# First MLP product by seven block products instead of eight, its result kept in DRAM

## The chip, the cores and the metric

The kernel runs on one core of a Trainium2 chip, as one launch. The metric is the device time in microseconds (us). Three runs of the kernel before took 3506.61 to 3510.11 us, with a median of 3507.81.

## The reference, cut to what matters

Two layer types work one after the other on x of 1024 tokens by 1024 features: `first_block` (two hybrid layers) and `second_block` (one layer with four branches, their merge and an MLP). Only the end of the second layer is touched:

```python
def rms_norm(x, gain): ...      # x * rsqrt(mean(x*x) + eps) * gain, over the features
...
    merged = merged + gate * (branches[i] @ w_branch_up[i])    # four branches
    x = x + rms_norm(merged @ w_out, norm_mix_post)

    h2 = rms_norm(x, norm_mlp_pre)
    u = jax.nn.relu(h2 @ w_mlp_in)                   # 1024 x 1024 by 1024 x 4096
    x = x + rms_norm((u * u) @ w_mlp_out, norm_mlp_post)   # by 4096 x 1024
```

## The kernel before

**Layout and products.** Everything is held transposed: a tile has 128 features (partitions) by 512 tokens, so that 1024 tokens are two halves. Each operand of a product is split into a high and a low part (`split`: ScalarE, written ACT, rounds the high part; VectorE, DVE, subtracts it from the source, which leaves the low part), and each product of two tiles is three matmuls, high by high, high by low and low by high (`mm3`, lines 113 to 115). `fm` adds such triples over the k tiles into one PSUM tile named `mm`. Weights come in blocks of 512 KB (128 x 1024) through `wload`: SP issues the load into `raw` (two buffers), ACT casts it to `whi` (line 104) and DVE subtracts it to `wlo` (line 105), each with two buffers too. `rnorm` makes a norm's scale for 512 tokens: TensorE (PE) adds a column of squares over the partitions (`tp`, line 198), DVE scales it (line 140), GpSimd (POOL) takes the root (line 141), PE spreads it over the partitions (`pv`, line 206).

**The stages at the end.** `merge` makes the four up-products and the gates, `proj` makes merged @ w_out for one half, and `norms` (before's lines 1797 to 1806) does the rest for that half: for each of eight tiles it loads a tile of the old x (`xo`, line 1802, two buffers), scales the product (line 1803, DVE), adds it to `xo` (line 1804, DVE), stores the new x as `x3` in DRAM (line 1805); after the eight, `norm_half` squares and adds them (lines 186 to 190), takes a second `rnorm`, and scales (line 219) and splits them to the operand H of the MLP.

**The MLP before.** `mlp` runs over eight chunks of 512 hidden features. In a chunk `hidden` makes four f tiles of h2 @ w_mlp_in for both halves, each tile 8 k x 3 = 24 matmuls of 128 x 512; ACT copies it (line 1840), DVE does max(t, 0)·t (line 1841) and it is split into M tiles. `project` then multiplies those by four blocks of w_mlp_out and adds each result to Y (line 1862, DVE; the first chunk is copied by ACT, line 1860). Nothing of u goes to DRAM. `finish` makes the last norm, adds x3 and stores out_t (lines 1881 to 1883). The two products are 32 x 2 x 24 = 1536 matmuls each.

**What sets the order.** The order of each engine's instructions is fixed when the kernel is built, by a scheduler that may take an instruction earlier or later than its place in the text; each engine then works its list in order. SP's list holds nearly all DMA issues, the weight loads, `xo` loads and stores among them. A DMA issue that has to wait for a buffer or for data holds up all that stands behind it in SP's list.

## Time and profile before

| What | us |
| --- | --- |
| Median of three runs | 3507.81 |
| Profiled execution, its own time | 3508.32 |
| Span of its instructions | 3506.5 |
| Last root of `norms` (half 1) to the last matmul of the MLP | 2776.0 to about 3486 of the span |
| Tail after the last matmul | 20.5 |

A profile lists for each engine what it did and when. PE is the matmul engine, PEld its weight loads, DVE VectorE, ACT ScalarE, POOL GpSimd, SP the engine that issues DMAs (SPq its queue). A busy figure counts the time in which an instruction of the engine is in flight; matmuls overlap, so that their mean duration is longer than the distance from the start of one to the start of the next. The granted clock says at what share of its full speed (2.4 GHz) TensorE was let run.

### The profile page before, as it was taken

The numbers are of one execution on the slowest core, as the hardware profiler recorded it, in microseconds if no ns is written. First come the engines' busy times: TensorE is split into PE (matmuls) and PEld (weight loads), VectorE is DVE, ScalarE is ACT, GpSimd is POOL, SyncE is SP. The second block draws the span as 40 slices with busy tenths as digits, with TensorE's granted clock in tenths as the row PEclk, the third lists the DMA queues.
The fourth block names the chain that finished last, engine by engine and source line by source line (L and its number), as shares of the span: only waits on it lengthen the run. The fifth ranks groups of instructions, "written<-read, shape, count | busy, mean of one in ns | idle before, by whom it ended". The sixth has DMA issues, their size and how long they took to land.

```text
span 3506.5 us, 45207 instructions
## 1 busy us (share of the span) xinstructions
PE 3369.9 (96%) x18181; PEld 2812.7 (80%) x18181; DVE 1966.9 (56%) x3418; ACT 1321.3 (38%) x2106; POOL 109.2 (3%) x132
## 2 busy tenths in 40 slices
PE   7999999999999999999999999999989899999997
...
GB/s 185 57 36 51 50 55 57 140 179 86 48 43 36 41 46 63 158 162 119 87 95 65 67 55 56 49 70 75 85 256 178 158 89 48 48 49 49 49 61 149
DMA packets 138707, 302.34 MB, mean 86 GB/s; under 512 B 23944, under 2 KB 41336, under 8 KB 137984
## 3 DMA queue, kind: packets, MB, share of 16 engines
...
q8 instruction: 143, 2.34, 0.3%
...
## 4 chain that ended last, share of the span: by engine, by line
PE 83%; DVE 5%; issue 5%; ACT 3%; DMA 3%; POOL 1%; SPq 0%; DVEq 0%; POOLq 0%; ACTq 0%
PE mm L113 21%; PE mm L114 21%; PE mm L115 21%; PE lg L388 2%; PE lg L389 2%; PE tp L512 2%; PE pv L113 1%; PE pv L206 1%; PE pv L114 1%; PE pv L115 1%; DMA S<-mix 1%; PE tp L198 1%; DVE wlo L105 1%; PE tp L1392 1%; ACT whi L104 1%
## 5 line engine op out<-in xcount | busy, mean ns | idle before, releaser
L113 PE MATMUL mm<-H,whi 128*128 128x512 f32 x2400 | 958.2, 400 | 26.9 <-DVE S L369 5.0
L115 PE MATMUL mm<-H,wlo 128*128 128x512 f32 x2400 | 949.4, 396 | 5.9 <-DVE wlo L105 5.7
L114 PE MATMUL mm<-H,whi 128*128 128x512 f32 x2400 | 949.8, 396 | 2.1 <-DVE H L105 2.1
L104 ACT CAST whi<-raw 128x1024 fp32r<-128x1024 f32 (+1 forms) x340 | 334.4, 984 | 860.3 <-PE mm L114 768.7
L105 DVE TENSOR_TENSOR wlo<-raw,whi 128x1024 fp32r<-128x1024 f32 (+1 forms) x340 | 387.4, 1140 | 421.6 <-ACT whi L104 409.9
L113 PEld LDWEIGHTS mm<-H,whi 128*128 128x128 f32 x2400 | 456.5, 190 | 125.5 <-ACT H L107 7.2
L115 PEld LDWEIGHTS mm<-H,wlo 128*128 128x128 f32 x2400 | 455.7, 190 | 104.2 <-DVE wlo L105 12.3
L114 PEld LDWEIGHTS mm<-H,whi 128*128 128x128 f32 x2400 | 456.2, 190 | 92.7 <-DVE H L105 2.9
L113 PE MATMUL mm<-whi,H 128*128 128x256 f32 x960 | 277.2, 289 | 3.9 <-DVE S L576 3.2
L114 PE MATMUL mm<-wlo,H 128*128 128x256 f32 x960 | 274.6, 286 | 3.1 <-DVE wlo L105 3.1
L115 PE MATMUL mm<-whi,H 128*128 128x256 f32 x960 | 273.7, 285 | 0.0
L113 PE MATMUL mm<-M,whi 128*128 128x512 f32 x640 | 249.5, 391 | 1.7 <-ACT whi L104 1.5
L115 PE MATMUL mm<-M,wlo 128*128 128x512 f32 x640 | 249.7, 390 | 0.2 <-DVE wlo L105 0.2
L114 PE MATMUL mm<-M,whi 128*128 128x512 f32 x640 | 249.5, 390 | 0.0
L113 PEld LDWEIGHTS mm<-whi,H 128*128 128x128 f32 x960 | 184.6, 192 | 6.8 <-issue 4.2
L114 PEld LDWEIGHTS mm<-wlo,H 128*128 128x128 f32 x960 | 184.8, 193 | 5.1 <-DVE wlo L105 4.2
L115 PEld LDWEIGHTS mm<-whi,H 128*128 128x128 f32 x960 | 184.6, 192 | 0.4
L489 DVE CUSTOM_DVE_ANT_0 lg<-lg,strip 128x1024 f32<-128x1024 f32 x128 | 155.2, 1234 | 25.8 <-PE lg L389 25.6
L1862 DVE TENSOR_TENSOR Y<-Y,mm 128x512 f32<-128x512 f32 x112 | 77.0, 687 | 159.1 <-PE mm L115 159.0
L493 ACT ACTIVATE L<-lg,mx 128x1024 f32<-128x1024 f32 x128 | 142.7, 1118 | 36.5 <-DVE mx L489 30.3
L113 PEld LDWEIGHTS mm<-M,whi 128*128 128x128 f32 x640 | 120.2, 188 | 28.0 <-ACT whi L104 1.9
L115 PEld LDWEIGHTS mm<-M,wlo 128*128 128x128 f32 x640 | 120.5, 188 | 25.6 <-DVE wlo L105 0.6
...
## 6 DMA issues: line engine op xcount, KB each, us to landing
raw<-in_w_in SPq DMA_DIRECT2D x106, 512.0 KB, 3.6
raw<-in_w_out SPq DMA_DIRECT2D x48, 512.0 KB, 4.0
raw<-in_w_gate SPq DMA_DIRECT2D x46, 512.0 KB, 3.5
raw<-in_w_mlp_in SPq DMA_DIRECT2D x40, 512.0 KB, 3.3
raw<-in_w_mlp_out SPq DMA_DIRECT2D x40, 512.0 KB, 3.2
...
```

The costliest lines, as they stand in the source:

```text
L104: nc.scalar.copy(hi, src)
L105: nc.vector.tensor_tensor(out=lo, in0=src, in1=hi.bitcast(F32), op=ALU.subtract)
L113: mm(out, lh, rh, start=start, stop=False)
L114: mm(out, lh, rl, start=False, stop=False)
L115: mm(out, ll, rh, start=False, stop=stop)
L198: self.nc.tensor.matmul(ss[:, n * i + j:n * i + j + 1], acc[:, j * P:(j + 1) * P], self.one, start=True, stop=True)
L388: mm(out, Q[m][qb // 4][:, sl], KH[m][half][:, o:o + kn], start=True, stop=False)
L389: mm(out, Q[m][qb // 4][:, sl], KL[m][half][:, o:o + kn], start=False, stop=not more)
L489: nc.vector.tensor_tensor_reduce(out=lg, in0=lg, in1=strip[:, w0:w0 + 1024], op0=ALU.add, op1=ALU.min, scale=-1.0, scalar=3.0e38, accum_ou ...
L493: nc.scalar.activation(pm, lg, AF.Exp, bias=mx, scale=-1.0, accum_out=sm)
L512: nc.tensor.transpose(tp[:, j, :], pm[:, kb * P:(kb + 1) * P], self.ident)
L1862: nc.vector.tensor_tensor(out=Y[d][half], in0=Y[d][half], in1=pt, op=ALU.add)
```

## The change

**First product.** The first MLP product is done in blocks. For a pair g of f tiles (f1 = 2g, f2 = 2g + 1; 16 pairs), the weights are a 2 x 2 matrix of blocks A11, A12 (f1, k tiles 0 to 3 and 4 to 7), A21, A22 (f2), and the operand is a 2 x 2 matrix B11, B21 (half 0, k tiles 0 to 3 and 4 to 7), B12, B22 (half 1). Seven block products of 4 k x 3 = 12 matmuls replace eight: A11·B11, A12·B21, S2·T2, S1·T1, S3·T3, A22·T4, S4·B22, with S1 = A21 + A22, S2 = S1 − A11, S3 = A11 − A21, S4 = A12 − S2 made on DVE for each pair (`side_weights`), and T1 = B12 − B11, T2 = B22 − T1, T3 = B22 − B12, T4 = T2 − B21 made once (`side_sums`, T1 and T2 on DVE, T3 and T4 on POOL). Each S, T, A22 is then split into high and low. DVE puts the products together with seven adds a pair (`add`).

**Order in the text.** For the first E = 8 pairs, A11·B11 and A12·B21, which need half 0 only, stand in a loop of their own between the steps of `norms` for half 1; this stretch is called stage A here. The main loop then does S2·T2 and the rest for all 16 pairs (and A11·B11 and A12·B21 for the last eight).

**u in DRAM.** `relu2` is now ACT twice (Relu, Square), and u goes to DRAM by 64 stores of 256 KB from SP. The second product runs over four chunks of 1024 rows, for which `inner` loads the 16 tiles of u again and splits them; the w_mlp_out blocks are laid out for that. In the last chunk all of half 0 comes ahead of half 1.

**norms.** The sum with `xo` is done by POOL instead of DVE (line 1815 in the new text), the squares are added as each tile is finished, and the scaling is one DVE instruction (line 1825) ahead of the plain split. The tail's tiles (`Y`, `M`, `xo`) share one pool of 54 buffers named S.

The diff, cut:

```diff
@@ norms
-            r = self.rnorm(acc, 1.0 / 1024.0)
-            for f in range(8):
-                xo = self.T("xo", 2)
-                nc.sync.dma_start(out=xo, in_=self.x2[f * P:(f + 1) * P, hs])
...
-                nc.vector.tensor_tensor(out=ys[f], in0=ys[f], in1=xo, op=ALU.add)
-                nc.sync.dma_start(out=self.x3[f * P:(f + 1) * P, hs], in_=ys[f])
-            res.append(self.norm_half(ys, self.n2[:, 16:24]))
+            order = [0, 4, 1, 5, 2, 6, 3, 7]
...
+            def add(fs):
+                for f in fs:
+                    xo = self.T("xo", 2)
+                    nc.sync.dma_start(out=xo, in_=self.x2[f * P:(f + 1) * P, hs])
+                    nc.vector.scalar_tensor_tensor(out=ys[f], in0=ys[f], scalar=self.n2[:, 8 + f:9 + f], in1=st["r"], op0=ALU.mult, op1=ALU.mult)
+                    nc.gpsimd.tensor_tensor(out=ys[f], in0=ys[f], in1=xo, op=ALU.add)
+                    nc.sync.dma_start(out=self.x3[f * P:(f + 1) * P, hs], in_=ys[f])
+                    self.sumsq_add(st["acc"], ys[f], f == 0)
...
+            def scale(fs):
+                for f in fs:
+                    X[f] = self.T("Y", 16)
+                    nc.vector.scalar_tensor_tensor(out=X[f], in0=ys[f], scalar=self.n2[:, 16 + f:17 + f], in1=st["r2"], op0=ALU.mult, op1=ALU.mult)
+                n2(half, fs, X)
+            pairs = [order[2 * i:2 * i + 2] for i in range(4)]
+            return X, [first] + [lambda p=p: add(p) for p in pairs] + [second] + [lambda p=p: scale(p) for p in pairs]
@@ new functions
+    def side_sums(self, b11, b21, b12, b22, use):
...
+        nc.vector.tensor_tensor(out=t1, in0=b12, in1=b11, op=ALU.subtract)
+        nc.vector.tensor_tensor(out=t2, in0=b22, in1=t1, op=ALU.subtract)
+        use("T2", t2)
+        use("T1", t1)
+        nc.gpsimd.tensor_tensor(out=t3, in0=b22, in1=b12, op=ALU.subtract)
+        use("T3", t3)
+        nc.gpsimd.tensor_tensor(out=t4, in0=t2, in1=b21, op=ALU.subtract)
+        use("T4", t4)
+        use("B22", b22)
...
+    def side_weights(self, src1, src2, whole):
...
+        if whole:
+            W["A11"], W["A12"] = self.block_weights(raw[0], 4)
+        s1 = sm(a21, a22, ALU.add)
+        s2 = sm(s1, a11, ALU.subtract)
+        part("S2", s2)
+        part("S1", s1)
+        part("S3", sm(a11, a21, ALU.subtract))
+        part("A22", a22)
+        part("S4", sm(a12, s2, ALU.subtract))
+        return W
@@ mlp, first product
+        def relu2(f, half, t):
+            u = self.T("ht", 2)
+            nc.scalar.activation(u, t, AF.Relu)
+            nc.scalar.activation(u, u, AF.Square)
+            nc.sync.dma_start(out=ud[f][half], in_=u)
...
+        for g in range(E + 1):
+            if g < E:
...
+                w11, w12 = self.block_weights(raw, 4)
+                S1[g] = copied(self.prod(w11, XS["B11"]))
+            if last is not None:
+                c11(*last)
+            last = (g, S1[g], w12) if g < E else None
+            for _ in range(2 if g in (0, 3) else 1):
+                if todo:
+                    todo.popleft()()
...
+        W = weights(0)
+        for g in range(NG):
+            f1, f2 = 2 * g, 2 * g + 1
+            s1 = S1[g] if g < E else copied(self.prod(W["A11"], XS["B11"]))
+            w = add(s1, self.prod(W["S2"], XS["T2"]))
+            if g >= E:
+                c11(g, s1, W["A12"])
+            t = add(w, self.prod(W["S1"], XS["T1"]))
+            p7 = self.prod(W["S3"], XS["T3"])
+            add(w, p7, w)
+            relu2(f2, 1, add(t, p7))
+            nextw = weights(g + 1) if g + 1 < NG else None
+            relu2(f2, 0, add(w, self.prod(W["A22"], XS["T4"]), w, ALU.subtract))
+            relu2(f1, 1, add(t, self.prod(W["S4"], XS["B22"]), t))
+            W = nextw
@@ mlp, second product
+            for k in range(8):
+                t = self.T("Y", 16)
+                nc.sync.dma_start(out=t, in_=ud[8 * ch + k][half])
+                hi, lo = (self.hpage(), self.hpage()) if half == 0 else (self.T("M", 32, F32R), self.T("M", 32, F32R))
+                self.split(hi, lo, t)
...
+        for ch in range(4):
+            U = [inner(ch, half) for half in range(2)]
+            if ch == 3:
+                break
             for d in range(8):
...
+                w = wload2(ch, d)
+                for half in range(2):
+                    project(ch, d, w, U[half], half)
```

**Order on SP in stage A.** First the rows of before, behind the first root of `norms` for half 1: L1802 loads a tile of the old x into `xo`, L1805 stores a tile of x3 (here called x).

```order
L1802 DMA xo_24100<-x_70 128x512
L1802 DMA xo_24105<-x_70 128x512
L1805 DMA x_14166<-Y_23892 128x512
L1802 DMA xo_24110<-x_70 128x512
L1805 DMA x_14166<-Y_23928 128x512
L1802 DMA xo_24115<-x_70 128x512
L153 DMA raw_24366<-in_w_mlp_out 128x1024
L1805 DMA x_14166<-Y_23964 128x512
L1805 DMA x_14166<-Y_24000 128x512
L1802 DMA xo_24120<-x_70 128x512
L1802 DMA xo_24125<-x_70 128x512
L153 DMA raw_24402<-in_w_mlp_out 128x1024
```

Now the same place in the new kernel: L1813 loads a tile of the old x into a tile of the pool S, L1816 stores x3, L1953 loads w_mlp_in, L1932 stores u.

```order
L1813 DMA S_24177<-x_70 128x512
L1813 DMA S_24183<-x_70 128x512
L1953 DMA raw_24303<-in_w_mlp_in 128x1024
L1816 DMA x_14166<-S_23823 128x512
L1816 DMA x_14166<-S_23965 128x512
L1813 DMA S_24231<-x_70 128x512
L1813 DMA S_24239<-x_70 128x512
L1953 DMA raw_24372<-in_w_mlp_in 128x1024
L1932 DMA u_24078<-N_24227 128x512
L1816 DMA x_14166<-S_23857 128x512
L1816 DMA x_14166<-S_24001 128x512
L1813 DMA S_24287<-x_70 128x512
```

What moved: the loads of the old x come in pairs, and each pair after the first stands behind the two stores of the pair before it, with a weight load and later a store of u in the same list.

**Order on DVE behind the second root of half 1.** Before: L140 is a step of the root, L219 scales a tile, L108 and L105 make low parts of H, M and the weights, L1841 is max(t, 0)·t.

```order
L140 TENSOR_SCALAR rn_24153<-tp_24154 128x4
L105 TENSOR_TENSOR wlo_24405<-raw_24402,whi_24404 128x1024
L219 TENSOR_TENSOR ht_24168<-Y_23822,pv_24161 128x512
L219 TENSOR_TENSOR ht_24174<-Y_23856,pv_24161 128x512
L1841 SCALAR_TENSOR_TENSOR M_24359<-M_24359 128x512
L108 SCALAR_TENSOR_TENSOR H_24167<-ht_24168,n_133,H_24166 128x512
L108 SCALAR_TENSOR_TENSOR H_24173<-ht_24174,n_133,H_24172 128x512
L219 TENSOR_TENSOR ht_24180<-Y_23892,pv_24161 128x512
L219 TENSOR_TENSOR ht_24186<-Y_23928,pv_24161 128x512
L105 TENSOR_TENSOR M_24363<-M_24359,M_24362 128x512
L108 SCALAR_TENSOR_TENSOR H_24179<-ht_24180,n_133,H_24178 128x512
L108 SCALAR_TENSOR_TENSOR H_24185<-ht_24186,n_133,H_24184 128x512
```

Now the end of the same stretch, up to the low part of S2 (S_24688), which the main loop's first product needs: L1825 scales, L1859 and L1860 make T1 and T2, L108 makes low parts, L1941 adds a product, L1888 makes S1 and S2.

```order
L1825 SCALAR_TENSOR_TENSOR S_24630<-S_24073,n_133,pv_24367 128x512
L1859 TENSOR_TENSOR S_24632<-S_24628,S_23780 128x512
L1860 TENSOR_TENSOR S_24633<-S_24630,S_24632 128x512
L108 TENSOR_TENSOR H_24657<-S_24630,H_24656 128x512
L108 TENSOR_TENSOR S_24639<-S_24633,S_24638 128x512
L108 TENSOR_TENSOR S_24643<-S_24632,S_24642 128x512
L108 TENSOR_TENSOR S_24648<-S_24634,S_24647 128x512
L108 TENSOR_TENSOR S_24653<-S_24635,S_24652 128x512
L1941 TENSOR_TENSOR S_24673<-H_24607,mm_24660 128x512
L1888 TENSOR_TENSOR S_24683<-raw_24681 128x512
L1888 TENSOR_TENSOR S_24685<-S_24683,raw_24679 128x512
L108 TENSOR_TENSOR S_24688<-S_24685,S_24687 128x512
```

What moved: each pair of half 1's tiles now takes nine DVE instructions (two scalings, two sums, five low parts) beside an add of a product, and all four pairs and two sums of weights stand ahead of the low part of S2, where before a product could start with the first scaled tile.

## Rows read from the trace of the kernel before

**Rows 1.** The page: busy time by engine; the chain that ended last, by engine.

```profile
PE 3369.9 (96%) x18181; PEld 2812.7 (80%) x18181; DVE 1966.9 (56%) x3418; ACT 1321.3 (38%) x2106; POOL 109.2 (3%) x132
PE 83%; DVE 5%; issue 5%; ACT 3%; DMA 3%; POOL 1%; SPq 0%; DVEq 0%; POOLq 0%; ACTq 0%
```

**Rows 2.** Stretches: length, then PE, PEld, DVE, ACT, POOL busy (count), clock, DMA share, GB/s.

```profile
2720.80:2776.00 55.20, 50.39 (x225) 40.52 (x224) 39.28 (x57) 26.60 (x40) 2.01 (x2) 0.97 0.47 153
2776.00:2860.00 84.00, 79.82 (x355) 64.73 (x355) 50.76 (x70) 37.77 (x56) 2.01 (x2) 0.98 0.40 132
2860.00:3420.00 560.00, 559.92 (x2470) 463.35 (x2469) 202.79 (x255) 120.41 (x164) 0.00 (x0) 1.00 0.16 52
3420.00:3486.00 66.00, 65.08 (x285) 52.98 (x283) 46.14 (x63) 23.73 (x33) 1.01 (x1) 0.97 0.46 162
3486.00:3506.50 20.50, 3.24 (x17) 2.75 (x16) 11.71 (x19) 0.63 (x1) 1.01 (x1) 0.61 0.27 103
```

**Rows 3.** Groups by line and shape, 2720.8 to 3506: busy us, mean ns | idle before.

```profile
L115 PE MATMUL mm<-M,wlo 128*128 128x512 f32 x572 | 223.3, 391 | 0.2 <-DVE wlo L105 0.2
...
L105 DVE TENSOR_TENSOR wlo<-raw,whi 128x1024 fp32r<-128x1024 f32 x86 | 105.3, 1224 | 146.6 <-ACT whi L104 146.3 <-issue 0.3
...
L104 ACT CAST whi<-raw 128x1024 fp32r<-128x1024 f32 x86 | 90.5, 1052 | 378.3 <-PE mm L114 376.7 <-issue 1.6
L1862 DVE TENSOR_TENSOR Y<-Y,mm 128x512 f32<-128x512 f32 x112 | 77.0, 687 | 159.1 <-PE mm L115 159.0
...
L104 ACT CAST M<-M 128x512 fp32r<-128x512 f32 x64 | 39.8, 621 | 68.6 <-DVE M L1841 68.6
...
L189 ACT ACTIVATE sq<-Y 128x512 f32<-128x512 f32 x35 | 21.9, 630 | 31.8 <-DVE Y L1862 15.9 <-DVE Y L1804 15.5 <-DVE acc L190 0.2
...
L1803 DVE SCALAR_TENSOR_TENSOR Y<-Y,n,pv 128x512 f32<-128x512 f32 x16 | 11.0, 742 | 4.7 <-PE pv L206 4.7
```

**Rows 4.** Timeline of the root of `norms`, half 1: start us, us, instruction [idle before].

```profile
2776.03 1.02 PE L198 MATMUL tp<-one,yacc 128*128 128x1 f32 x8
...
2777.41 1.01 POOL L141 TENSOR_TENSOR rn<-rn,mhalf 128x4 f32<-128x4 f32 x1 [27.72 <-DVE rn L140]
...
2778.47 1.16 PE L206 MATMUL pv<-c_ident,rn 128*128 128x128 f32 x8 [0.83 <-POOL rn L141]
...
2779.66 1.41 DVE L1803 SCALAR_TENSOR_TENSOR Y<-Y,n,pv 128x512 f32<-128x512 f32 x2 [2.34 <-PE pv L206]
...
2780.99 1.29 DVE L1804 TENSOR_TENSOR Y<-Y,xo 128x512 f32<-128x512 f32 x2
...
2782.19 3.37 DVE L1803 SCALAR_TENSOR_TENSOR Y<-Y,n,pv 128x512 f32<-128x512 f32 x5
```

**Rows 5.** SP's timeline in the same place, and the tile `xo` from issue to landing.

```profile
2781.70 0.93 SPq L1805 DMA_DIRECT2D x<-Y  x2
2782.68 0.95 SPq L1802 DMA_DIRECT2D xo<-x  x2
...
DMA to landing us min/median/max: 3.3/3.7/5.8
```

**Rows 6.** POOL's groups by line and shape, whole span: its instruction nearest in size.

```profile
L362 POOL MEMSET S<- 64x512 f32 x16 | 8.3, 521 | 17.1 <-PE lg L388 6.3 <-DVE N L219 3.3 <-ACT L L104 2.9
```

**Rows 7.** PE's timeline after a wait, and the stretch's granted clock.

```profile
2791.28 0.80 PE L115 MATMUL mm<-H,wlo 128*128 128x512 f32 x1 [1.81 <-DVE wlo L105]
2791.88 0.63 PE L113 MATMUL mm<-H,whi 128*128 128x512 f32 x1
2792.30 0.63 PE L114 MATMUL mm<-H,whi 128*128 128x512 f32 x1
...
2780.00:2800.00 20.00, 17.04 (x68) 13.31 (x67) 17.75 (x27) 9.78 (x15) 0.00 (x0) 0.91 0.65 219
```

**Rows 8.** DMA issues: count, KB each, median us from issue to landing.

```profile
raw<-in_w_mlp_in SPq DMA_DIRECT2D x40, 512.0 KB, 3.3
raw<-in_w_mlp_out SPq DMA_DIRECT2D x40, 512.0 KB, 3.2
```

More of the change, by code (lines that the diff above doesn't have):

```diff
@@ new lines, in mixed @@
+        def mixed(half, fs, X):
+            i = fs[0]
+            self.side_sums(X0[i], X0[4 + i], X[i], X[4 + i], lambda n, t: self.keep(XS, n, i, t))
+        _, steps = norms(1, ys[1], accs[1], mixed)
+        return XS, steps
+    def side_sums(self, b11, b21, b12, b22, use):
+        nc = self.nc
+        t1, t2, t3, t4 = (self.T("Y", 16) for _ in range(4))
+        nc.vector.tensor_tensor(out=t1, in0=b12, in1=b11, op=ALU.subtract)
[7 more added lines that the diff above has]
+        use("B22", b22)
@@ new lines, in block_weights, with prod @@
+    def block_weights(self, raw, nb):
+        hi = self.wp.tile([P, 2 * nb, P], F32R, tag="whi", bufs=N_HI, name=self.nm("whi"))
+        lo = self.wp.tile([P, 2 * nb, P], F32R, tag="wlo", bufs=N_HI, name=self.nm("wlo"))
+        self.split(hi, lo, raw)
+        w = [(hi[:, k], lo[:, k]) for k in range(2 * nb)]
+        return w[:nb], w[nb:]
+    def prod(self, w, X):
+        out, n = self.ps("mm"), len(w)
+        for k in range(n):
+            self.mm3(out, w[k][0], w[k][1], X[k][0], X[k][1], k == 0, k == n - 1)
+        return out
@@ L1886, in mlp, with norm @@
-        for ch in range(last):
-            for halves in ((0,), (1,)) if ch == 0 else ((0, 1),):
-                project(ch, hidden(ch, halves), halves)
-        project(last, hidden(last, (0,)), (0,))
-        U = hidden(last, (1,), finish(0, olds(0)))
-        X = olds(1)
-        project(last, U, (1,))
-        for fn in finish(1, X):
-            fn()
+                nc.sync.dma_start(out=X[d], in_=self.x3[d * P:(d + 1) * P, hs])
+            st = {}
+            def norm():
+                st["r"] = self.rnorm(accs[half], 1.0 / 1024.0)
@@ new lines, in scale, with wload2 @@
+            def scale(d):
+                y = Y[d][half]
+                nc.vector.scalar_tensor_tensor(out=y, in0=y, scalar=self.n2[:, 24 + d:25 + d], in1=st["r"], op0=ALU.mult, op1=ALU.mult)
+                nc.vector.tensor_tensor(out=y, in0=y, in1=X[d], op=ALU.add)
+                nc.sync.dma_start(out=out[d * P:(d + 1) * P, hs], in_=y)
+            return [norm] + [lambda d=d: scale(d) for d in range(8)]
+        def wload2(ch, d):
+            return self.wload(self.seg("w_mlp_out", (ch * 8 + d) * 1024, 8, 128), 8, 128)
@@ L1922, in second_block @@
                 self.fill(len(self.fills) - NLATE)
-            end_banks()
-            with self.banks("tail", 4, 0, 1, 2), self.phase("tail"):
-                H2 = self.merge(brd)
-                self.mlp(H2, out)
+        end_banks()
+        self.uni = {"S": NT, "L": 0, "N": 5}
+        with self.banks("tail", 4, 0, 1, 2), self.phase("tail"):
+            XS, steps = self.merge(brd)
+            self.mlp(XS, steps, out)
 def _woff():
@@ L2094, in _arrays @@
     a["w_mlp_in"] = _lay(g["w_mlp_in_2"][0], [(128 * j, 128) for j in range(32)])
[L2095 removed]
+    a["w_mlp_out"] = np.concatenate([_lay(g["w_mlp_out_2"][0, 1024 * c:1024 * c + 1024], [(128 * j, 128) for j in range(8)]) for c in range(4)], 1)
     return a
```

136 lines of the change are left out of this document (83 added, 53 removed).

## The prediction, made before the changed kernel had run

> **What bounds the kernel now.** I read the page first, then the stretches of the MLP, then the groups of instructions in them, and last the timeline of the place where the two versions part. On the page PE is busy for 96% of the span and makes 83% of the chain that ended last [rows 1]. The stretches say how tight that is in the part that changes. From 2860 to 3420 us PE is busy for 559.92 of 560.00 us at a clock of 1.00, with 2470 matmuls [rows 2]: one matmul starts every 560.00 / 2470 = 0.2267 us. The 391 ns in the groups [rows 3] is the time that one is in flight, not its price, since they overlap; by that figure the change would seem to bring 192 × 0.391 = 75 us, by the distance of starts it can bring 43.5. In the same stretch DVE is busy for 203 us of 560 and the DMAs for 16%, so there is room beside PE.
>
> At the edges PE waits a little. The MLP runs in the trace from 2776.0, the root of `norms` for half 1 [rows 4], to 3486.0, 710.0 us. From 2776 to 2860 there are 355 matmul records, 32 of them the small ones of the two roots (16 each), so 323 × 0.2267 = 73.2 us of work in 84.0: 10.8 us lost. From 3420 to 3486 it is 285 − 16 = 269, so 61.0 in 66.0: 5.0 lost [rows 2]. The sum is made against the profiled execution, 3508.32 us, which is 0.5 us above the median of the runs.
>
> **1. Matmuls removed.** The first product has 16 pairs × 7 × 12 = 1344 matmuls for 1536. That is 192 × 0.2267 = **−43.5 us** if PE stays as full as it was. PE issues one queue, so this is exact only where operands are in time; the next terms are about that.
>
> **2. Stage A.** Up to the same root PE has the same work in both. Thirteen of stage A's 8 × 24 = 192 matmuls stand ahead of that root, 179 behind it: 179 × 0.2267 = 40.6 us of cover. They need half 0 alone. The next product, S2·T2, needs half 1's norm to be wholly done, since all seven sets are made from it; before, a product could begin with the first scaled tiles. So I add up the chain from 2776.0 to S2·T2.
> - First root: 2779.66 − 2776.03 = 3.6 us to the first scaling, which takes 0.74 [rows 3, 4].
> - Residual sums in four pairs. In SP's list of the new kernel a pair's loads of the old x stand behind the two stores of the pair before. A round is two POOL sums, the second store's issue (0.46), and an old tile from issue to landing, 3.7 [rows 5]. POOL did no 128x512 sum in the trace. Its nearest row is a memset of 64x512, 0.52 us [rows 6], which reads nothing; a sum reads two streams, so I take twice that, 1.04. Bounds are 0.52 and 1.6 (three streams for one). A round is then 2.08 + 0.46 + 3.7 = 6.2, three of them 18.7, and the last pair's sums 2.1: 3.6 + 0.7 + 18.7 + 2.1 = 25.1.
> - The last square and its sum, 0.63 + 0.69 [rows 3]: 26.4. Second root 3.6: 30.0.
> - DVE from there to the low part of S2 has 47 instructions: 8 scalings at the distance of starts (3.37 − 0.74) / 4 = 0.66 [rows 4], 3 low parts of weights at 1.22 [rows 3], and 36 sums of 128x512 at 1.29 − 0.69 = 0.60 [rows 3, 4]: 5.3 + 3.7 + 21.6 = 30.6. For each pair it also waits for ACT's first cast (0.62) and for POOL's T4 (1.04 less a sum beside it), about 1 us: 4. Together 64.6.
> - Semaphore steps from engine to engine: in the first root they were 0.05 to 0.4 us each; with four rounds and four pairs, some 5.
>
> So S2·T2 starts some **70 us** after 2776.0, not 40.6: PE idles for about 29 us in stage A. Bounds: with a POOL sum of 0.52 and no waits 59, with a sum of 1.6 75.
>
> **3. The main loop.** For the first eight pairs PE has 60 matmuls, 13.6 us, and DVE 15 instructions of 0.69 [rows 3], 10.3 us; for the others 84 matmuls, 19.0 us, and DVE 12.2. ACT has two passes for each u, six or eight, and five casts or so, under 9 us of about 0.62 each. The two weight blocks of the next pair are loaded in this time; one lands in 3.3 us [rows 8]. In SP's list the second stands behind the store of the last u of the pair before, and I make its slack about 2 us. So PE is the bound here and the DVE work is hidden; if it is not, a pair costs the overhang (rival C).
>
> **4. u in DRAM.** 64 stores and 64 loads of 256 KB, 33.5 MB in about 640 us, 52 GB/s. Half 0 and half 1 of a chunk are split by 16 casts and 16 sums, under 11 us of DVE beside 384 matmuls, 87 us of PE. The DVE instruction max(t, 0)·t has gone. I price this at nothing except at the edges: the first chunk waits for the last buffers of the first product, 2 us, and each later chunk start 0.5.
>
> **5. Half 0 and the end.** `norms` for half 0 has the same SP rounds, but 192 matmuls of `proj` for half 1 are there as cover, as before (a loss of 11.5 us for 55.2 [rows 2], partly the merge): 0, between −2 and +6. The tail behind the last matmul, 20.5 us [rows 2], stays.
>
> **The sum.** Behind stage A are 2880 − 192 = 2688 matmuls: 609.4 us. Losses there: half clock after the idle time, 1.3 (after a wait of 1.81 us six matmuls started 0.43 apart instead of 0.23 and the clock was 0.91 in that stretch [rows 7]); hand-over 2; three chunk starts 1.5; the last stretch as before, 5. Together 10. 70 + 609.4 + 10 = 689.4 for 710.0: −20.6. As a balance: −43.5 from the matmuls, +29 for stage A, −6 from losses that were there before. 3508.3 − 20.6 = 3487.7, on the scale of the median **3487 us**.
>
> **Rivals.**
> - **A. POOL and DVE hold each other up.** If a POOL sum and a DVE sum cannot run at once, the eight sums of T3 and T4 lie fully on the DVE chain, 8 × 1.04 = 8.3, and the residual sums lose some 2: +10, **3497**. For: in stage A nearly every DVE instruction has two operands in SBUF. Against: no row shows it; POOL does almost nothing beside DVE in the trace (109 us in all [rows 1]).
> - The Trainium skill, "SBUF — State Buffer", section "Who interferes with whom", states this as a rule: a DVE instruction with two inputs in SBUF contends with a GpSimd instruction that reads SBUF, and the loser blocks for the whole of it. The trace of before shows no case of it. The skill's "GPSIMD Engine Reference", section "3.1 Elementwise — side-by-side cycle accounting", has 4497 ns for a sum of 2048 columns, an estimate of 1.12 us for 512, and keeps DVE as the place for elementwise sums; by it the sum would come to 3488 without the lock and 3499 with it.
> - **B. Stage A is covered.** If POOL's sums, the loads and DVE's instructions overlap more than I add them, S2·T2 starts when the 192 matmuls end: −43.5, **3465**. For: DVE idles in the first 26 us of my chain. Against: that chain is latency, fixed by the order on SP.
> - **C. Weights late in the main loop.** If the second block's load or DVE's sums miss by 1.5 us a pair: 15 × 1.5 = 22, **3509**, no change. Against: 10.3 of 13.6 us.
> - **D. Slower: the chunk starts of the second product.** SP's list mixes loads of u, which wait for buffers that PE's products free, with weight loads. If a weight load stands behind a u load that waits for the product before to end, PE waits for buffer 5.4 (a product of 24), landing 3.3, cast 1.05 and low part 1.22: 11 us for each of three chunks, 33: **3520**. It decides when a chunk's weights are issued later than the start of the product before. Against: at the start of a chunk two weight blocks lie ahead of the u loads.
> - **E.** The change does not save what it says: the PE list is 192 rows shorter, so hardly.
>
> **Chances.** Forecast 0.47 (own range 3478 to 3494), A 0.25, B 0.10, C 0.06, D 0.10, E 0.02. Faster by over 0.2% (7 us, about what a measurement can tell from no change): the forecast, A and B, 0.82. Within 0.2%: C and E, 0.08. Slower: D, 0.10. The range goes from just above B, 3466, to the upper end of A and part of C, 3505; D is left out, with the ends of B and C.
>
> **What will show it.** PE's start of S2·T2 about 70 us behind the last of the `tp` before stage A, with an idle PE ahead of it put down to DVE's low part; DVE idle between POOL's sums, with `xo` rounds of 6 us; a POOL sum of 1.0 us, and DVE's sums beside it at 0.69 (forecast) or up to 1.7 (A); from S2·T2 on PE at 0.2267 us a matmul, with DVE at 75% of a small pair (C: a wait for the low part of an S in each pair); no wait over 2 us at chunk starts (D: 11). The forecast is wrong if the rounds of `xo` take far from 6 us, since the loss in stage A rests on them and on DVE's 47 instructions.

## The result: slower, and where the time is

The changed kernel takes 3527.7 us (median of four runs, 3524.9 to 3539.2) against 3508.9 us (four runs): ratio **1.0067**, 95% interval 1.0055 to 1.0079. The forecast was 3487, the range 3466 to 3505. The profiled execution took 3526.5 us, its span is 3524.6.

The page of the changed kernel, which answers to [rows 1]: busy time by engine, and the chain that ended last by engine.

```profile
PE 3341.4 (95%) x17989; PEld 2781.5 (79%) x17989; DVE 2030.7 (58%) x3526; ACT 1398.4 (40%) x2254; POOL 146.8 (4%) x156
PE 77%; issue 10%; DVE 5%; ACT 3%; DMA 3%; POOL 1%; SPq 0%; POOLq 0%; DVEq 0%; ACTq 0%
```

PE has 28.5 us less to do than before (3341.4 for 3369.9) and yet the span is 18 us longer. To see where, I put four events beside each other that both kernels have in the same order: the last `tp` of the last branch, ahead of `merge`; ACT's copy of the eighth projection of half 0 (L1793 before, L1796 after); the `tp` of the root of half 1; the last matmul. The first S2·T2 stands only in the new kernel. All from the timelines of PE and ACT, in us.

| Event | Before | After | After less before |
| --- | --- | --- | --- |
| Last `tp` ahead of `merge` | 2561.58 | 2561.69 | +0.1 |
| Copy of the eighth projection, half 0 | 2718.84 | 2743.53 | +24.7 |
| `tp` of the root, half 1 | 2776.03 | 2810.64 | +34.6 |
| First S2·T2 | - | 2882.30 | - |
| Last matmul | 3485.75 | 3504.35 | +18.6 |

So the new MLP is quicker than the old one, 693.7 us from the root to the last matmul for 709.7. But 34.6 us are lost ahead of it, in two stretches in which PE has the same work: 631 and 234 matmul records in either kernel.

**First loss: the up-products of half 0, 24.6 us.** Who PE waited for (us in total, times, longest), first the changed kernel from 2560 to 2745 us, then the kernel before from 2561.6 to 2718.8:

```profile
PE mm L116 <- DVE S L1783: 17.4, 6, 2.9
PE mm L116 <- ACT H L107: 7.7, 1, 7.7
```

```profile
PE mm L113 <- ACT H L104: 3.7, 1, 3.7
PE mm L113 <- DVE Y L1780: 2.7, 4, 1.4
PE mm L114 <- DVE H L105: 2.1, 1, 2.1
```

Of the 24.6 us, 14.7 are longer waits for the scalings (17.4 for 2.7) and 1.9 longer waits for `H` (7.7 for 5.8). Another 8.1 us are matmuls that take longer: PE is busy for 156.0 us in the stretch, and was for 147.9.

One of the six waits, on PE's timeline (start, duration, instruction, idle before):

```profile
2603.55 0.39 PE L118 MATMUL mm<-H,wlo 128*128 128x512 f32 x1
2606.84 0.47 PE L116 MATMUL mm<-H,whi 128*128 128x512 f32 x1 [2.90 <-DVE S L1783]
2607.15 0.53 PE L117 MATMUL mm<-H,whi 128*128 128x512 f32 x1
2607.48 0.63 PE L118 MATMUL mm<-H,wlo 128*128 128x512 f32 x1
2607.91 0.63 PE L116 MATMUL mm<-H,whi 128*128 128x512 f32 x1
```

and what VectorE did meanwhile:

```profile
2604.87 1.23 DVE L108 TENSOR_TENSOR wlo<-raw,whi 128x1024 fp32r<-128x1024 f32 x1 [3.27 <-ACT whi L107]
2606.01 1.88 DVE L1783 SCALAR_TENSOR_TENSOR S<-S,mm 128x512 f32<-128x512 f32 x3
```

PE starts the last matmul of a step of four products at 2603.55 and then finds no free PSUM tile `mm`: the four hold products that the scalings L1783 have not read. These stand on VectorE's list behind the low part of a block of weights two steps ahead, whose buffer PE frees only at the end of that very step. So the cast (1.04 us), the low part (1.23) and the first scaling come one after the other while PE stands. After five of the six waits some eight matmuls start 0.43 us apart instead of 0.23; after the first, at 2588 us, none do. The granted clock of that stretch of the changed kernel, and of the one that answers to it in the kernel before (columns as in [rows 2]):

```profile
2590.00:2640.00 50.00, 35.49 (x120) 27.12 (x119) 31.64 (x47) 8.38 (x10) 0.00 (x0) 0.84 0.49 165
```

```profile
2590.00:2620.00 30.00, 28.55 (x123) 22.40 (x122) 29.47 (x46) 8.01 (x10) 0.00 (x0) 1.00 0.86 295
```

It took 50 us to do what took 30. A step is 10.2 us long (casts of weights at 2593.58, 2603.80, 2613.99, ...) and was 6.0 (2591.93 to 2621.70 for five).

**Second loss: `norms` of half 0, 9.9 us** (from the eighth copy to the root of half 1: 67.1 us for 57.2). Who PE waited for there in the changed kernel, 2743.5 to 2810.6:

```profile
PE mm L118 <- DVE wlo L108: 4.6, 1, 4.6
PE mm L116 <- ACT S L1796: 2.8, 2, 2.0
PE pv L209 <- POOL rn L144: 2.0, 2, 1.2
```

and at which clock (columns as in [rows 2]; the nearest row there has 0.97):

```profile
2743.50:2810.60 67.10, 57.74 (x234) 45.98 (x232) 39.87 (x50) 27.53 (x44) 14.78 (x10) 0.87 0.41 131
```

The low part that PE waits 4.6 us for stands on VectorE's list behind four squares, which wait for POOL's sums with xo. It starts at 2759.39, beside the next such sum, and takes 2.28 us.

**Stage A came out as forecast, by other means.** S2·T2 starts 71.7 us behind the root (forecast 70), after an idle time of 16.4 us:

```profile
2882.30 0.79 PE L116 MATMUL mm<-S,S 128*128 128x512 f32 x1 [16.35 <-ACT S L107]
```

In the whole of stage A PE is busy for 47.5 us (columns as in [rows 2]), so that it idles for 24 us, where the forecast had 29:

```profile
2810.60:2882.30 71.70, 47.49 (x212) 36.25 (x211) 55.66 (x70) 37.13 (x60) 25.79 (x18) 0.91 0.40 129
```

The rounds are there: on SP the stores of x3 (L1816) start 6.2 and 6.9 us apart, answering to [rows 5]:

```profile
2816.42 1.58 SPq L1816 DMA_DIRECT2D x<-S  x2
2818.04 0.93 SPq L1813 DMA_DIRECT2D S<-x  x2
...
2822.62 1.57 SPq L1816 DMA_DIRECT2D x<-S  x2
...
2829.51 1.57 SPq L1816 DMA_DIRECT2D x<-S  x2
```

But a POOL sum, which I took at 1.04 us, is slower, and VectorE is slower beside it. POOL's and VectorE's groups in the changed kernel (busy us, mean ns | idle before), 2720 to 3524 us:

```profile
L1815 POOL TENSOR_TENSOR S<-S,S 128x512 f32<-128x512 f32 x16 | 22.3, 1423 | 17.7 <-DMA S<-x 13.9 <-DVE S L1814 2.1 <-DVE N L193 1.7
...
L193 DVE TENSOR_TENSOR N<-N,N 128x512 f32<-128x512 f32 x14 | 13.4, 959 | 7.3 <-ACT N L192 7.1
...
L1865 POOL TENSOR_TENSOR S<-S,S 128x512 f32<-128x512 f32 x4 | 6.9, 1733 | 3.9 <-DVE S L1860 3.2 <-POOL S L1863 0.7
L1863 POOL TENSOR_TENSOR S<-S,S 128x512 f32<-128x512 f32 x4 | 6.4, 1588 | 18.9 <-ACT N L1931 13.3 <-DVE S L1825 5.5
L1860 DVE TENSOR_TENSOR S<-S,S 128x512 f32<-128x512 f32 x4 | 5.6, 1402 | 0.1
...
L1859 DVE TENSOR_TENSOR S<-S,S 128x512 f32<-128x512 f32 x4 | 2.7, 682 | 0.0
```

L1859 and L1860 are the same operation. In three of the four pairs L1860 starts inside POOL's T3 and takes 1.63 to 1.65 us; in the first pair a low part of weights meets T3 in its place, and L1860 takes 0.68. On the timelines of POOL and of VectorE one of the three:

```profile
2855.72 1.60 POOL L1863 TENSOR_TENSOR S<-S,S 128x512 f32<-128x512 f32 x1 [5.55 <-DVE S L1825]
```

```profile
2856.22 1.65 DVE L1860 TENSOR_TENSOR S<-S,S 128x512 f32<-128x512 f32 x1
```

VectorE's sum starts inside POOL's, which ends at 2857.32, and itself ends at 2857.87, 0.55 us later: it stood until POOL was done. The other rows of the new tail in this trace say the same. Fourteen VectorE sums of 128x512 with both operands in SBUF start inside a POOL sum, and each ends 0.55 us behind it; three low parts of 128x1024 do, and each ends 1.08 us behind it. It holds the other way round too: thirteen POOL sums start inside such a VectorE instruction, and each ends 1.12 to 1.16 us behind it, after 1.55 to 2.14 us instead of 1.27 to 1.30. VectorE's scalings L1814, which read one tile from SBUF and one (`pv`) from PSUM, take 0.73 or 0.74 us beside a POOL sum as without one. Five of them take 3.38 us here and took 3.37 with POOL idle [rows 4]:

```profile
2750.03 10.56 POOL L1815 TENSOR_TENSOR S<-S,S 128x512 f32<-128x512 f32 x7 [2.13 <-DMA S<-x]
```

```profile
2749.15 3.38 DVE L1814 SCALAR_TENSOR_TENSOR S<-S,n,pv 128x512 f32<-128x512 f32 x5 [2.34 <-PE pv L209]
```

**The main loop is as forecast.** From 2900 to 3100 us PE is never idle, 884 matmul records in 200 us, 0.2262 us each, at VectorE 65% busy:

```profile
2900.00:3100.00 200.00, 200.00 (x884) 165.68 (x883) 129.94 (x198) 97.21 (x160) 0.00 (x0) 1.00 0.37 124
```

### The profile page after: what moved, and what is told of

Same layout as the page of the kernel before. It is cut to its first block, busy times and chain, and to the rows that moved or that the text cites. A ratio compares the mean times of both kernels' runs of the same rounds, so it can differ in the third digit from the quotient of the medians.

```text
span 3524.6 us, 45450 instructions
## 1 busy us (share of the span) xinstructions
PE 3341.4 (95%) x17989; PEld 2781.5 (79%) x17989; DVE 2030.7 (58%) x3526; ACT 1398.4 (40%) x2254; POOL 146.8 (4%) x156
## 4 chain that ended last, share of the span: by engine, by line
PE 77%; issue 10%; DVE 5%; ACT 3%; DMA 3%; POOL 1%; SPq 0%; POOLq 0%; DVEq 0%; ACTq 0%
PE mm L116 20%; PE mm L117 19%; PE mm L118 19%; PE lg L391 2%; PE lg L392 2%; PE tp L515 2%; DVE wlo L108 1%; PE pv L116 1%; PE pv L209 1%; PE pv L117 1%; DMA S<-mix 1%; PE pv L118 1%; PE tp L201 1%; PE tp L1395 1%; ACT whi L107 1%
## 5 line engine op out<-in xcount | busy, mean ns | idle before, releaser
L116 PE MATMUL mm<-H,whi 128*128 128x512 f32 x2272 | 912.0, 402 | 51.7 <-DVE S L1783 17.4
L118 PE MATMUL mm<-H,wlo 128*128 128x512 f32 x2272 | 903.2, 398 | 6.7 <-DVE wlo L108 6.6
L117 PE MATMUL mm<-H,whi 128*128 128x512 f32 x2272 | 902.7, 397 | 0.9 <-DVE H L108 0.8
L107 ACT CAST whi<-raw 128x1024 fp32r<-128x1024 f32 (+3 forms) x316 | 308.9, 979 | 724.2 <-PE mm L117 583.2
L108 DVE TENSOR_TENSOR wlo<-raw,whi 128x1024 fp32r<-128x1024 f32 (+3 forms) x316 | 361.3, 1145 | 391.5 <-ACT whi L107 380.7
L116 PEld LDWEIGHTS mm<-H,whi 128*128 128x128 f32 x2272 | 434.6, 191 | 150.0 <-issue 20.4
L117 PEld LDWEIGHTS mm<-H,whi 128*128 128x128 f32 x2272 | 434.0, 191 | 88.8 <-DVE H L108 3.4
L116 PE MATMUL mm<-S,whi 128*128 128x512 f32 x576 | 228.8, 400 | 11.4 <-ACT S L107 6.0
L118 PE MATMUL mm<-S,wlo 128*128 128x512 f32 x576 | 229.4, 398 | 8.1 <-DVE wlo L108 8.0
L117 PE MATMUL mm<-S,whi 128*128 128x512 f32 x576 | 229.2, 398 | 0.5 <-DVE S L108 0.5
L492 DVE CUSTOM_DVE_ANT_0 lg<-lg,strip 128x1024 f32<-128x1024 f32 x128 | 155.3, 1235 | 25.7 <-PE lg L392 25.3
L116 PEld LDWEIGHTS mm<-S,whi 128*128 128x128 f32 x576 | 110.4, 192 | 40.0 <-ACT S L107 8.2
L108 DVE TENSOR_TENSOR S<-S,S 128x512 fp32r<-128x512 f32 x152 | 104.5, 708 | 62.0 <-ACT S L107 61.0
L118 PEld LDWEIGHTS mm<-S,wlo 128*128 128x128 f32 x576 | 110.3, 192 | 34.9 <-DVE wlo L108 12.6
```

The costliest lines, as they stand in the source:

```text
L107: nc.scalar.copy(hi, src)
L108: nc.vector.tensor_tensor(out=lo, in0=src, in1=hi.bitcast(F32), op=ALU.subtract)
L116: mm(out, lh, rh, start=start, stop=False)
L117: mm(out, lh, rl, start=False, stop=False)
L118: mm(out, ll, rh, start=False, stop=stop)
L492: nc.vector.tensor_tensor_reduce(out=lg, in0=lg, in1=strip[:, w0:w0 + 1024], op0=ALU.add, op1=ALU.min, scale=-1.0, scalar=3.0e38, accum_ou ...
```

## The experiments

The runs of before that stand beside them have medians of 3507.0 (e1 to e4), 3509.5 (e5 to e8) and 3509.8 us (e9 to e11). Single runs of one kernel scatter by up to 15 us about their median there, and the part ahead of `merge`, which no edit touches, by 9 us between profiles. So the verdicts rest on stretches of the profiled executions between the events of the table above, which scatter less (*up* is 155.3 to 157.5 us in the ten kernels without the shared pool): *up* from the last `tp` ahead of `merge` to the eighth copy, *norms* from there to the root of half 1, *A* from the root to S2·T2, *rest* from there to the last matmul.

| Kernel | Median us | Ratio to before (95%) | up | norms | A | rest |
| --- | --- | --- | --- | --- | --- | --- |
| before | 3508.9 | 1 | 157.3 | 57.2 | 709.7 with the rest | - |
| after | 3527.7 | 1.0067 (1.0055 to 1.0079) | 181.8 | 67.1 | 71.7 | 622.1 |
| e1_pool | 3550.2 | 1.0115 (1.0096 to 1.0134) | 182.2 | 63.4 | 719.0 with the rest | - |
| e2_sep | 3494.8 | 0.9964 (0.9948 to 0.9980) | 156.5 | 66.4 | 71.0 | 615.1 |
| e3_sep_dve | 3488.2 | 0.9941 (0.9918 to 0.9964) | 155.3 | 65.8 | 68.3 | 614.8 |
| e4_dve | 3523.3 | 1.0041 (1.0025 to 1.0057) | 181.7 | 61.6 | 70.6 | 624.1 |
| e5_t2 | 3487.6 | 0.9940 (0.9917 to 0.9963) | 156.3 | 66.2 | 63.2 | 614.6 |
| e6_int | 3491.0 | 0.9953 (0.9940 to 0.9966) | 155.3 | 66.9 | 71.0 | 614.6 |
| e7_sep34 | 3491.9 | 0.9947 (0.9930 to 0.9963) | 157.5 | 66.8 | 69.6 | 614.1 |
| e8_best | 3482.4 | 0.9919 (0.9893 to 0.9945) | 156.9 | 66.8 | 60.3 | 615.6 |
| e9_bestd | 3481.4 | 0.9919 (0.9898 to 0.9940) | 156.0 | 57.8 | 59.3 | 617.7 |
| e10_old0 | 3485.4 | 0.9927 (0.9907 to 0.9948) | 157.3 | 66.2 | 59.3 | 617.5 |
| e11_bestn | 3485.3 | 0.9934 (0.9915 to 0.9953) | 156.2 | 67.6 | 59.7 | 615.6 |

### The shared pool: e1_pool and e2_sep

My theory (M) was that the common pool S of 54 buffers changed the order on VectorE in `merge`, perhaps by taking away the limit of 16 buffers Y that the loads of gates had to wait for. The rival (R) was that something else new in the tail did it. e1_pool puts the pool into the kernel before; as in the changed kernel the tail then stands outside the block that holds the buffers of the branches:

```diff
-            end_banks()
-            with self.banks("tail", 4, 0, 1, 2), self.phase("tail"):
-                H2 = self.merge(brd)
-                self.mlp(H2, out)
+        end_banks()
+        self.uni = {"S": 54, "L": 0, "N": 5}
+        with self.banks("tail", 4, 0, 1, 2), self.phase("tail"):
+            H2 = self.merge(brd)
+            self.mlp(H2, out)
```

> The kernel before with one part of the change alone: the tail's tiles (Y, M, xo) share one pool S of 54 buffers, the rest is as before (eight products, u kept in SBUF, sums with xo on VectorE). Its VectorE list then has, in the first eight steps of the up-products, the low part of the weights of step f+2 ahead of the four scalings of step f+1, as in the changed kernel. Theory M (that order makes TensorE wait for PSUM buffers): the up stage of half 0 takes 10.2 us a step for 6.1, so 3508.9 + 24.7 = about 3533. Rival R (the shared pool costs nothing by itself, the loss in the merge comes from what else is new in the tail): 3509, within 3 us.

e2_sep takes it out of the changed kernel, by two pools of 54 buffers together, Y for most of what the kernel before had in Y (and the sums of weights) and S for the rest:

```diff
+            elif tag in ("Y", "ws", "wh", "wl") and "Y" in self.uni:
+                tag, bufs = "Y", self.uni["Y"]
             elif n <= 512:
                 tag, bufs = "S", self.uni["S"]
...
-            y = self.T("Y", 16)
+            y = self.T("Y" if half == 0 else "M", 16)
...
-                t = self.T("Y", 16)
+                t = self.T("M", 16)
                 nc.sync.dma_start(out=t, in_=ud[8 * ch + k][half])
...
-        self.uni = {"S": NT, "L": 0, "N": 5}
+        self.uni = {"S": 38, "Y": 16, "L": 0, "N": 5}
```

> The changed kernel with the shared pool split in two: Y (16 buffers: gates, up-products, sums, weight sums) and S (38: the rest). The VectorE list of the up-products is then as in the kernel before. Theory M: the 24.7 us of the merge go, 3527.7 - 24.7 = 3503. Rival R: the merge stays at 10.2 us a step and the time within 3 us of 3527.7.

Measured: *up* is 182.2 us in e1_pool, as in the changed kernel (181.8), and 156.5 in e2_sep, as in the kernel before (157.3). Who PE waited for in that stretch, first e1_pool, then e2_sep:

```profile
PE mm L113 <- DVE S L1780: 17.4, 6, 2.9
PE mm L113 <- ACT H L104: 7.7, 1, 7.7
```

```profile
PE mm L118 <- ACT H L109: 4.1, 1, 4.1
PE mm L118 <- DVE Y L1785: 2.8, 4, 1.5
```

M holds and R falls: the shared pool brings the loss, and two pools take it away with all else that is new left in, the place of the tail too. That it works through the loads of gates no run shows. VectorE's list at that place, first of the kernel before, then of e1_pool (wlo: low part of weights; L1780: scaling of a product):

```text
L1780 SCALAR_TENSOR_TENSOR Y_22494<-Y_22416,mm_22487 128x512
L1780 SCALAR_TENSOR_TENSOR Y_22503<-Y_22417,mm_22496 128x512
L1780 SCALAR_TENSOR_TENSOR Y_22513<-Y_22418,mm_22506 128x512
L1782 TENSOR_TENSOR Y_22503<-Y_22503,Y_22494 128x512
L1780 SCALAR_TENSOR_TENSOR Y_22523<-Y_22419,mm_22516 128x512
L1782 TENSOR_TENSOR Y_22513<-Y_22513,Y_22503 128x512
L105 TENSOR_TENSOR wlo_22598<-raw_22595,whi_22597 128x1024
```

```text
L105 TENSOR_TENSOR wlo_22599<-raw_22596,whi_22598 128x1024
L1780 SCALAR_TENSOR_TENSOR S_22495<-S_22417,mm_22488 128x512
L1780 SCALAR_TENSOR_TENSOR S_22504<-S_22418,mm_22497 128x512
```

One row has moved past six, and it costs 4 us a step. e1_pool misses its 3533 by 17 us: the pool costs the old kernel more further on (6.2 us in *norms*, 9.3 behind the root); the cause of that stays open. e2_sep is 3494.8 for 3503 expected; its *rest* is 7 us shorter too, 615.1 for 622.1, so the pool cost the changed kernel about 32 us in all, 25 of them in the up-products.

### The sums with xo: e3_sep_dve and e4_dve

The edit, once on e2_sep (e3) and once on the changed kernel (e4):

```diff
-                    nc.gpsimd.tensor_tensor(out=ys[f], in0=ys[f], in1=xo, op=ALU.add)
+                    nc.vector.tensor_tensor(out=ys[f], in0=ys[f], in1=xo, op=ALU.add)
```

> As e2_sep, and in norms the sums with xo (line 1815 of the changed kernel, 16 of 128x512) are done by VectorE instead of GpSimd. Theory P (in norms of half 0 the weights' low parts stand behind squares that wait for GpSimd's sums of 1.5 us, which makes TensorE wait 4.6 us and run at half clock after it): the 9.9 us of norms of half 0 go, and in stage A each round is some 1.8 us shorter: e2_sep less 10 to 17, 3486 to 3493. Rival Q (the loss there comes from the order on SP, stores of x3 ahead of weight loads, whoever does the sums): within 4 us of e2_sep.

> The changed kernel with the shared pool as it is, and only the sums with xo on VectorE. Theory M and P, which add up: 3527.7 less 10 to 17, 3511 to 3518, with the merge still at 10.2 us a step. Rival Q: within 4 us of 3527.7.

Measured: *norms* goes from 67.1 to 61.6 in e4, but only from 66.4 to 65.8 in e3. In e3 the wait for a low part is still there. Both kernels' stage A is 1 to 3 us shorter. e3's median lies in the range that theory P gave, but the stretches hold only 3.6 us of it, so that is luck; e4's is 4.4 us under the changed kernel's, between P and Q. So theory P, that POOL's slow sums make the 9.9 us, is not right as it stands: they are one part at most. Rival Q, the order on SP, is not shown either, see e6 and e9.

### T2 first: e5_t2

Per pair VectorE now makes T1, T2 and T2's low part only; the other low parts stand behind the sums of weights. T1, T3, T4 go into the buffers of their operands, and the scaled tiles of half 1 into pool S.

```diff
-        def mixed(half, fs, X):
-            i = fs[0]
-            self.side_sums(X0[i], X0[4 + i], X[i], X[4 + i], lambda n, t: self.keep(XS, n, i, t))
+        late = []
+        def mixed(half, fs, X):
+            i = fs[0]
+            b11, b21, b12, b22 = X0[i], X0[4 + i], X[i], X[4 + i]
+            t2 = self.T("Y", 16)
+            nc.vector.tensor_tensor(out=b11, in0=b12, in1=b11, op=ALU.subtract)
+            nc.vector.tensor_tensor(out=t2, in0=b22, in1=b11, op=ALU.subtract)
+            self.keep(XS, "T2", i, t2)
+            nc.gpsimd.tensor_tensor(out=b21, in0=t2, in1=b21, op=ALU.subtract)
+            nc.gpsimd.tensor_tensor(out=b12, in0=b22, in1=b12, op=ALU.subtract)
+            late.append((b11, b12, b21, b22))
...
+        def rest():
+            for k, n in enumerate(("T1", "T3", "T4", "B22")):
+                for i in range(4):
+                    self.keep(XS, n, i, late[i][k])
...
         W = weights(0)
+        self.rest()
```

> As e2_sep, and in stage A VectorE makes T2 of all four pairs first and the low parts of T1, T3, T4 and B22 behind the sums of the weights S1 and S2. Theory V (the start of S2.T2 hangs on the number of VectorE instructions behind the second root, of which 20 to 25 instead of 47 now stand ahead of it): S2.T2 starts 10 to 14 us earlier behind the root of half 1 than in e2_sep (71.0 us), some of which is given back by the later products of the first pair; the time is e2_sep less 4 to 10. Rival W (the stage hangs on the loads of the old x or on TensorE's own 179 matmuls): within 3 us of e2_sep.

Measured: A is 63.2 us for 71.0, and the rest is not longer (614.6 for 615.1). Theory V holds: the start of S2·T2 hangs on how many VectorE instructions stand ahead of it. It brought 7.8 us, less than the 10 to 14 expected, and nothing was given back.

### The steps of norms between the projections: e6_int

```diff
-        for fn in steps:
-            fn()
+        plan = {0: 2, 1: 2, 2: 2, 3: 2, 4: 2}
+        todo = deque(steps)
         for f in range(8):
             proj(f, 1, ys[1], accs[1])
+            for _ in range(plan.get(f, 0)):
+                todo.popleft()()
```

> As e2_sep, and the steps of norms of half 0 stand in the text between the projections of half 1 instead of ahead of them, so that on VectorE the low parts of the next w_out blocks stand ahead of the sums of squares. Theory D (in norms of half 0 TensorE waits 4 to 7 us for a low part that is queued behind six sums of squares, and runs at half clock after it): the stretch from the eighth projection of half 0 to the root of half 1 goes from 66.4 to 57 to 60 us, and the time is e2_sep less 6 to 9. Rival Q (stores of x3 ahead of the weight loads on SP): the same wait in another place, within 3 us of e2_sep.

Measured: *norms* 66.9 us, no shorter. Who PE waited for in it:

```profile
PE tp L203 <- DVE N L195: 4.1, 1, 4.1
PE mm L120 <- DVE wlo L110: 3.0, 1, 3.0
```

The low part now stands ahead, but the `tp` of the second root stands on PE's list and waits 4.1 us for sums of squares that are late instead. Theory D was half of it.

### T3 and T4 on VectorE: e7_sep34

```diff
-        nc.gpsimd.tensor_tensor(out=t3, in0=b22, in1=b12, op=ALU.subtract)
+        nc.vector.tensor_tensor(out=t3, in0=b22, in1=b12, op=ALU.subtract)
...
-        nc.gpsimd.tensor_tensor(out=t4, in0=t2, in1=b21, op=ALU.subtract)
+        nc.vector.tensor_tensor(out=t4, in0=t2, in1=b21, op=ALU.subtract)
```

> As e2_sep, and T3 and T4 are made by VectorE (8 sums more of 0.6 us) instead of GpSimd. Theory L (a GpSimd sum holds up VectorE for most of its 1.6 us, since low parts next to it take 1.8 to 2.3 us for 0.7 to 1.2): S2.T2 starts 2 to 5 us earlier behind the root of half 1 than in e2_sep (71.0 us). Rival N (no hold-up, VectorE's longer instructions have another cause): it starts some 5 us later.

Measured: A is 69.6 us for 71.0, with eight instructions more on VectorE, 5.5 us of work at 0.69. VectorE's T1, next to the moved sums, first in e2_sep and then in e7_sep34 (columns as in [rows 3]):

```profile
L1861 DVE TENSOR_TENSOR Y<-Y,Y 128x512 f32<-128x512 f32 x4 | 4.9, 1219 | 0.0
```

```profile
L1861 DVE TENSOR_TENSOR Y<-Y,Y 128x512 f32<-128x512 f32 x4 | 2.8, 692 | 0.0
```

The hold-up is real (theory L): with POOL's sum gone the same instruction is back at 0.69 us. The gain, 1.3 us, is below the 2 to 5 expected.

### All together: e8_best to e11_bestn

e8_best is e5, e6 and e7 on e2_sep; T3 and T4 are made on VectorE behind T2, just ahead of their low parts. e9_bestd has the sums with xo on VectorE too (the edit of e3). e11_bestn is e8_best without the edit of e6. e10_old0 is e9_bestd without it, and with half 0's squares behind all its sums. The new lines of e8_best, and then of e10_old0:

```diff
-            nc.gpsimd.tensor_tensor(out=b21, in0=t2, in1=b21, op=ALU.subtract)
-            nc.gpsimd.tensor_tensor(out=b12, in0=b22, in1=b12, op=ALU.subtract)
-            late.append((b11, b12, b21, b22))
+            late.append((b11, b12, b21, b22, t2))
...
                 for i in range(4):
+                    b11, b12, b21, b22, t2 = late[i]
+                    if n == "T3":
+                        nc.vector.tensor_tensor(out=b12, in0=b22, in1=b12, op=ALU.subtract)
+                    elif n == "T4":
+                        nc.vector.tensor_tensor(out=b21, in0=t2, in1=b21, op=ALU.subtract)
                     self.keep(XS, n, i, late[i][k])
```

```diff
-                    self.sumsq_add(st["acc"], ys[f], f == 0)
+                    if half:
+                        self.sumsq_add(st["acc"], ys[f], f == 0)
...
             def second():
+                if half == 0:
+                    for f in order:
+                        self.sumsq_add(st["acc"], ys[f], f == 0)
```

> e2_sep with the edits of e5_t2, e6_int and e7_sep34 together (T3 and T4 on VectorE behind the low parts of T2). Theories V, D and L add up: e2_sep less 14 to 22, about 3475 where e2_sep is 3495. If one of them is wrong, its share is missing.

> As e8_best, and the sums with xo on VectorE too, so that GpSimd has nothing but the roots. Theory L (GpSimd's sums hold up VectorE): the stretch from the eighth projection of half 0 to the root of half 1, 66.8 us in e8_best, is 2 to 5 us shorter, and stage A 0 to 3: e8_best less 2 to 8. Rival O (that stretch is set by where the low parts and the small products of the second root stand in the lists, whoever does the sums): within 3 us of e8_best.

> As e9_bestd, but norms of half 0 in the text as in the kernel before: all eight sums with xo first, then all squares, and the whole ahead of the projections of half 1. Theory O: the stretch from the eighth projection of half 0 to the root of half 1 is 57 to 60 us as in the kernel before (57.2). Rival S (the one shared list of SP or the smaller pool makes it long, whatever the order of the sums): 64 us or more, as in the others.

> As e8_best, with the steps of norms of half 0 ahead of the projections again as in the changed kernel. Theory D took the wait for a low part away and got one for the second root's sums in its place (e6_int): the stretch stays at 66 to 67 us and the time within 3 us of e8_best. If the interleaving did help, it is 3 us or more slower.

Measured: e8_best takes 3482.4 us, 12.4 under e2_sep, which is short of the 14 to 22 expected (14.9 when each is taken from the runs of before beside it); its A is 60.3, its *norms* still 66.8, so theory D's share is missing. In e9_bestd *norms* falls to **57.8**, about the value of the kernel before, 9.0 us for the 2 to 5 expected. With the sums on VectorE but ahead of the projections (e3, e10) it is 66 (61.6 in e4, on the one pool); between the projections but on POOL (e6, e8) it is 67; with neither (e2, e11) 66 to 68; with both 57.8. So both edits have to be there at once. The waits say why, as far as they go: low parts of weights have to stand early enough on VectorE's list (e3 and e10 wait for one, 5.4 and 5.3 us at the longest), and the sums have to be quick enough that the `tp` of the second root doesn't wait on PE's (e6 and e8 wait 4.1 and 4.5 us there). Who PE waited for in this stretch of e9_bestd:

```profile
PE pv L211 <- POOL rn L146: 3.4, 2, 1.7
PE mm L118 <- ACT whi L109: 2.9, 2, 1.7
PE mm L120 <- DVE wlo L110: 0.6, 1, 0.6
```

Theory O as I put it for e10 (the old order of sums and squares is enough) falls: 66.2, not 57 to 60. Its rival S, that the list of SP or the smaller pool makes the stretch long whatever the order, falls with e9's 57.8. e11 is 2.9 us above e8, inside its 3, with *norms* at 67.6 for 66 to 67.

Why the kernel before has 57.2 with the text of e10 stays open, and one rival is untested. In e10's list the eight scalings and eight sums with xo stand ahead of the first low part of weights after the first root, then the eight scalings and low parts of `H` ahead of a later one, for which PE waits 5.3 us:

```profile
2762.05 2.36 DVE L110 TENSOR_TENSOR wlo<-raw,whi 128x1024 fp32r<-128x1024 f32 x2
```

```profile
2763.32 0.79 PE L120 MATMUL mm<-S,wlo 128*128 128x512 f32 x1 [5.33 <-DVE wlo L110]
```

In the kernel before, where `xo` has two buffers, VectorE waits for xo loads and low parts stand between the sums (at 2733.54, 2737.05, 2742.48 us). No run gave `xo` its two buffers back in the new kernel. e1_pool, with the old text and the shared pool, already has 6.2 of the 9.9 us, so the pool may be behind much of this loss as well.

For e9's total the expectation was e8_best less 2 to 8; the medians differ by 0.9, within the scatter, and I rest on the stretch alone. e9_bestd is faster than both kernels: 0.9919 of before (0.9898 to 0.9940), 28 us.

## Why the prediction was wrong

Against its own sum, in the profiled execution (3487.7 forecast, 3526.5 measured):

| Step | Forecast us | Measured us | Miss |
| --- | --- | --- | --- |
| Up-products of `merge` | not in the sum | 181.8 for 157.3 before | +24.6 |
| 5, `norms` of half 0 | 0, -2 to +6 | 67.1 for 57.2 before | +9.9 |
| 2, stage A to S2·T2 | 70, bounds 59 to 75 | 71.7 | +1.7 |
| 1, 3, 4, from S2·T2 to the last matmul | 619.4 | 622.1 | +2.7 |
| 5, tail | 20.5 | 20.25 | -0.2 |

- **The step that failed is the one sentence that ended the sum early:** that up to the root of half 1 PE has the same work in both, from which I took the same time. The work is the same; the order on VectorE isn't, and I had compared the lists only from that root on for VectorE. The part of the change that I read as bookkeeping, one pool instead of several, moves instructions in `merge`, long before the MLP. It is two thirds of the miss (e1_pool, e2_sep), and no rival had it.
- **Step 5 was mis-sized:** I put it at 0 and named as cover 192 matmuls of the projections; it measured 9.9. There is cover, but VectorE's list is in order, and a block of weights whose low part stands behind the squares, or behind other steps of the norm, is late however much PE could do. That both edits of e9 bring the 57 us back is shown; what part of the loss the shared pool has is not (e1_pool: 6.2).
- **Step 1 held.** 192 matmuls fewer at 0.2267 us, and not at the 391 ns of [rows 3], is what the main loop shows. PE's busy time fell by 40.2 us from the root of half 1 on. Over the span it fell by only 28.5, since it rose by 8.1 in the up-products and by 5.3 in `norms` of half 0, where the granted clock fell.
- **Step 2 held in its sum and not in its parts, which is luck.** The rounds are 6.2 to 6.9 us. The POOL sum was taken from a memset at 1.04 and measured 1.42, 1.59 and 1.73 in the means of its three lines, the last two at and beyond my upper bound of 1.6. The 4 us of VectorE's waits for ACT and POOL were not there; instead VectorE was held up by POOL's sums, by some 9 us. The lower bound of 59 doesn't follow from its terms either: with a POOL sum of 0.52 and without the 4 us they give 61.4, and 56.4 without the 5 us of steps between engines as well. e5_t2 shows that the count of VectorE's instructions was the right thing to count.
- **Rival A had the right mechanism and nearly the right price.** From the root of half 1 to S2·T2 the VectorE instructions that met a POOL sum are, added up from the rows, 9.3 us longer than the same ones alone, 8.0 beside T3 and T4 and 1.3 in the squares, for its 8.3 and 2. e7 agrees: it moves T3 and T4 for a net gain of 1.3, which with 5.5 us more of VectorE work is a hold-up of about 7 us. Stage A came out only 1.7 us over the forecast all the same: the 4 us of waits were not there, and some 3.6 us more are missing in places that no run parts. The Trainium skill, "SBUF — State Buffer", section "Who interferes with whom", states this rule, and the trace agrees: L1860 takes 1.63 to 1.65 us where it starts inside a POOL sum and 0.68 where it doesn't. The Trainium skill's "GPSIMD Engine Reference", section "3.1 Elementwise — side-by-side cycle accounting", led to an estimate of 1.12 us for a POOL sum of 512 columns; the shortest here took 1.27 us and the median 1.30 (L1815), so the measurement decides.
- **Rival D, the only slower one, didn't come.** At 3140 to 3270 us, the start of the second product, the longest wait is 1.9 us (`H` from ACT), and at no chunk start 11.
- **Rivals B and C** fell as well: PE was idle for 16.4 us ahead of S2·T2, and no pair of the main loop waited.
